# Reordering the HGRN stage of a two-block transformer kernel: gate columns first, query products on VectorE, head pairs staggered, a VectorE matrix-vector product spread through the stage

## The chip, the cores and the metric

The kernel runs on one core of one Trainium2 chip. The metric is device time in microseconds (us) of one execution. TensorE (PE in the rows) does the matrix products, VectorE (DVE), ScalarE (ACT) and GpSimd (POOL) the elementwise work, and SyncE (SP) issues the weight transfers. Each engine runs its own instructions strictly in the order in which they were written.

## What is computed

The reference is two transformer blocks on 256 tokens of width 1024. The change touches only the first mixer of the first block, HGRN2, a gated linear recurrence over 8 heads of 128 key columns:

```python
def hgrn2_mixer(u, w_in, w_out, lb, o_gain):
    q, z_f, v, g = jnp.split(u @ w_in, [...], axis=-1)
    q = jax.nn.silu(q)
    sig = jax.nn.sigmoid(z_f)
    f = lb + (1 - lb) * sig
    log_f = jnp.log(jnp.maximum(f, MIN_FORGET))
    k = (1 - lb) * (1 - sig)
    ...
    attn = jnp.einsum('bthd,btshd,bshd->bhts', qc, decay, kc)
    o = (jnp.einsum('bhts,bshv->bthv', attn, vc)
         + jnp.einsum('bthd,bhdv->bthv', qc * jnp.exp(b), state))
    ...
    o = o * lax.rsqrt(jnp.mean(o * o, axis=-1, keepdims=True) + NORM_EPS) * o_gain
    o = o * jax.nn.silu(g)
    return o @ w_out
```

Beside it the block needs `mod = silu(c) @ mod_w + mod_b`, six matrix-vector products (gemv) of 1024 x 1024 each. The third one (number 2) gates the residual after the mixer, numbers 3 and 4 shift and scale the feed-forward part that follows.

## The kernel before, in words

The core keeps activations transposed (features on partitions, 256 tokens on the free axis) and streams every weight once from memory, in units of 512 KB. A unit is loaded into one of 7 raw buffers by SyncE, then split in two by `emit_conv`: ScalarE casts it to `w_hi` (L193), VectorE subtracts to get `w_lo` (L195), and TensorE multiplies three times for each block, hi·hi, hi·lo and lo·hi (L258 to L260, `mm3`). At most three units are converted ahead of TensorE.

The program is a list of steps, and `run` writes their instructions in the order of the list; before each step `pump` writes the transfers and conversions that have become possible. Nothing is rescheduled afterwards. Inside the HGRN stage the list is the hand-written string `HG_ORDER`. Its names, where the first digit is the pair of heads (0 to 3) and the second a part or level:

- `f20 f21 f30 f31`: gate columns of pairs 2 and 3 on TensorE; `fa fb fc`: their sigmoid in three parts (VectorE, ScalarE, ScalarE `gates_of`). The gates of pairs 0 and 1 come out of the first products (`lin_first`), which stand ahead of `HG_ORDER`, through `ev_f`.
- `d`: `hg_d`, the floor of f at 1e-30 and the product QP = q·f; `t`: `hg_t`, six products of neighbouring f, of neighbouring products and so on, a tree of GpSimd products (L854).
- `s`: `hg_s`, the within-pair products of keys and queries at one of nine levels. Level 8 needs k and q, level 7 needs QP, and the lower levels need keys and queries that `u`, `hg_u`, has scaled with the tree: the key half on GpSimd (L871, L865), the query half on VectorE (L872, L866). So `u06` follows `s07` and precedes `s06`, down to `s00`. `c`: `hg_c`, masked copies of the products of two levels on VectorE.
- `v0` to `v7`: value columns; `w`, `wa wb wc`: output gate; `pv sq st r n m o ol`: products with the values, norm, gate, split in hi and lo; `a0` to `a5`: first part of the output projection.
- `y2x y3x y4x` (x = 0 to 7): the gemv numbers 2, 3 and 4, one 512 KB unit each. 3 and 4 run on TensorE (L523, eight small products). Number 2 runs on VectorE: `gemv_w` multiplies each unit by one column of the condition and adds it to two 128x512 tiles `ga` (L515 for the first unit, L517 for the other seven), and `q2` then sums over partitions on TensorE (L523), `z2` adds the bias.

A `w_lo` conversion that is written behind a waiting instruction on VectorE waits with it, and TensorE then waits for the conversion.

Of the kernel before, what the change touches and what calls it, by code (L numbers as in the profile page):

```python
# [13 lines left out]
AF = mybir.ActivationFunctionType  # L14
OP = mybir.AluOpType
# [31 lines left out]
tr5 o0 y46 y47 pv4 tr6 o1 o2 z3 q4 pv5 pv6 tr7 o3 pv7 z4 o4 o5  # L47
"""
HG_ORDER = """
d0 d1 t0 t1 y30 f20 f21 s08 s18 s07 s17 c00 c10 u06 u16 y31 f30 fa2 s06 s16 u05 u15 y32 fb2 f31 s05 s15 c01 c11  # L50
u04 u14 fc2 y33 v0 fa3 s04 s14 u03 u13 fb3 y34 v1 s03 s13 c02 c12 u02 u12 fc3 d2 y35 v2 s02 s12 u01 u11 d3 t2 t3
y36 v3 s01 s11 u00 u10 s28 s27 s38 s37 y37 v4 s00 s10 u26 u36 c20 c30 z3 v5 s26 s36 u25 u35 pv0 sq0 y40 v6 s25
s35 c21 c31 u24 u34 st0 r0 y41 v7 s24 s34 u23 u33 n0 pv1 sq1 y42 w00 s23 s33 c22 c32 u22 u32 st1 r1 y43 w01 s22
s32 u21 u31 n1 y44 w10 wa0 s21 s31 u20 u30 wb0 y45 w11 wc0 s20 s30 m0 y46 wa1 w20 o0 wb1 ol0 pv2 sq2 wc1 y47 y20
w21 m1 st2 r2 pv3 sq3 z4 y21 w30 o1 ol1 wa2 n2 st3 r3 y22 y23 w31 wb2 wc2 m2 n3 y24 a0 wa3 o2 ol2 wb3 y25 a1 wc3
m3 y26 a2 o3 ol3 y27 a3 q2 a4 z2 a5
"""


# [72 lines left out]
def kernel(ctx: ExitStack, tc: tile.TileContext, x, c, mod_w, mod_b, norm_mix, norm_ffn,  # L132
# [9 lines left out]
    PE, DV, SC, GP, SY = nc.tensor, nc.vector, nc.scalar, nc.gpsimd, nc.sync  # L142
# [24 lines left out]
    def ph(w, name, bufs=2, dt=F32, tag=None):  # L167
        return phase["p"].tile([P, w], dt, name=name, tag=tag or name, bufs=bufs)

    def small(w, name, bufs=2, dt=F32):  # L170
        return wk.tile([P, w], dt, name=name, tag=name, bufs=bufs)
# [464 lines left out]
    st0 = {}  # L636
# [89 lines left out]
    T = {}  # L726
    wa = a_w_in[0]
# [7 lines left out]
        T["v"] = [v[:, 0:D], v[:, D:2 * D]]  # L735

    steps.append(Step(start_hgrn))
    qf, qf_evac, g_steps = [], [], []
    for j in range(4):
        def ev_q(p, j=j):  # L740
            SC.activation(T["q"][:, 2 * j:2 * j + 2].rearrange("p k t -> p (k t)"), p, AF.Silu)
        qf_evac.append(ev_q)
    def gates_of(sg, j):
        for m in range(2):
            h = 2 * j + m
            s_ = sg[:, 256 * m:256 * m + 256]
            if j > 1:
                SC.activation(T["f"][:, h], s_, AF.Identity, bias=lb[:, h:h + 1], scale=one_lb[:, h:h + 1])
                SC.activation(T["k"][:, h], s_, AF.Identity, bias=one_lb[:, h:h + 1], scale=cols[:, 24 + h:25 + h])
                continue  # L750
            DV.tensor_scalar(T["f"][:, h], s_, one_lb[:, h:h + 1], lb[:, h:h + 1], op0=OP.mult, op1=OP.add)
            DV.tensor_scalar(T["k"][:, h], s_, cols[:, 24 + h:25 + h], one_lb[:, h:h + 1], op0=OP.mult, op1=OP.add)

    def pair(n, j):
        return T[n][:, 2 * j:2 * j + 2].rearrange("p k t -> p (k t)")
# [9 lines left out]
    for j in range(2):  # L765
        def ev_f(p, j=j):
            sg = small(512, "sig", 2)
            SC.activation(sg, p, AF.Sigmoid)
            gates_of(sg, j)
        qf_evac.append(ev_f)  # L770
    items = {}
    for j in range(2, 4):
        def ev_f2(p, j=j):
# [19 lines left out]
    def lin_first(h, a, u):  # L793
# [12 lines left out]
        for n in (2 * a, 2 * a + 1):  # L806
# [7 lines left out]
            if h == 3:  # L814
                qf_evac[n](first[n])

    lf = [[Step(lambda u, h=h, a=a: lin_first(h, a, u), [unit_A(wa, 256 * h, (0, 512, 1024)[a], 2, 512)], 2.6)
           for a in range(3)] for h in range(4)]
    for h in range(4):
        steps += [Step(lambda h=h: u0_part(h, LOOK if h == 3 else 1))] + [Step(start_w)] * (h == 3) + lf[h][:1]  # L820
# [17 lines left out]
    DP, QP, SB = {}, {}, {}  # L838

    def hg_d(p):  # L840

        f = pair("f", p)
        DV.tensor_scalar(f, f, 1e-30, None, op0=OP.max)
        QP[p] = ph(512, "qp", 4)
        GP.tensor_mul(QP[p], pair("q", p), f)
        DP[p] = {1: f}

    def hg_t(p):

        d, o = ph(504, "dp", 4), 0  # L850
        for h in (2, 4, 8, 16, 32, 64):
            two = DP[p][h // 2].rearrange("p (n s) -> p n s", s=2)
            DP[p][h] = d[:, o:o + 512 // h]
            GP.tensor_mul(DP[p][h], two[:, :, 0], two[:, :, 1])  # L854
            o += 512 // h
# [120 lines left out]
    def S_(f, *a, cost=1.0):  # L976
        return Step(lambda: f(*a), [], cost)

    def item(key, f, *a):
        items[key] = [S_(f, *a)]  # L980

    LS = ((8, 7), (6, 5), (4, 3))
    for p in range(4):
        for n, f in (("d", hg_d), ("t", hg_t), ("m", hg_m), ("pv", hg_pv), ("sq", hg_sq), ("st", hg_st), ("r", hg_r), ("n", hg_n), ("o", hg_o),
                     ("ol", hg_ol)):
            item(f"{n}{p}", f, p)
        for l in range(9):
# [273 lines left out]
    items = {}  # L1261
# [570 lines left out]
    items = {"sca": [Step(b2_scale)], "col": [Step(b2_cols)], "cx": [S_(c_x)]}  # L1832
# [4 lines left out]
    for i, it in enumerate(mixers):  # L1837
        kind, p = it
# [49 lines left out]
```

## Time and profile before

| what | value |
|---|---|
| time, median of 3 runs (lowest to highest) | 1169.14 us (1168.44 to 1169.78) |
| time of the profiled execution | 1170.95 us |
| span of its trace, first to last instruction | 1169.2 us |
| mean granted TensorE clock | 0.991 of full speed |
| TensorE busy | 1121.8 us (96%) |
| TensorE weight loads | 1037.5 us (89%) |
| VectorE busy | 759.7 us (65%) |
| ScalarE busy | 572.0 us (49%) |
| GpSimd busy | 138.3 us (12%) |
| chain that ended last, share of TensorE | 78% |

The profiled execution lies 1.81 us above the median of the runs. The span is 1.75 us shorter than that execution's own time; what lies outside the trace is not touched by the change. "Busy" of TensorE is modelled, since matmuls overlap; an idle time that the rows give in square brackets is the time from the end of the work before, and behind the arrow stands what ended it. The first products run up to about 68 us of the span, the HGRN stage up to about 211 us. A granted clock of 1.00 is 2.4 GHz, the other level is 1.2 GHz; a stretch that shows 0.61 had some of both.

### The profile page before, as it was taken

To read this page: it belongs to the slowest core of one execution; us is meant where nothing else is said; L and a number is where in the kernel's file an instruction comes from. 1 tells how busy PE (TensorE), PEld (TensorE's weight loads), DVE (VectorE), ACT (ScalarE), POOL (GpSimd) and SP (SyncE) were. 2 spreads that over 40 slices of the span, in tenths; PEclk is the share of its full clock that TensorE was granted. 3 is DMA by queue.
4 is the path that set the end of the run, shared out by engine and by line. 5 is a ranking of instruction groups with operands and counts; after the bars stand their busy time and mean duration, and the time that the engine had idled before them with its cause. 6 is when DMAs were issued, how large, how long until landed. Compare 5 with 4: busy or idle time off the path is not lost.

```text
span 1169.2 us, 23616 instructions
## 1 busy us (share of the span) xinstructions
PE 1121.8 (96%) x9689; PEld 1037.5 (89%) x9689; DVE 759.7 (65%) x1233; ACT 572.0 (49%) x913; POOL 138.3 (12%) x205
## 2 busy tenths in 40 slices
PE   6988998999999999999999999999998999999997
PEld 4976786899999978888999999988898999999997
DVE  3557477677867678885645544666856766766766
ACT  3355263544434556563534434645556544544454
POOL 4035310000000000250000000013322100000000
PEclk9999898999999999999999999999999999999999
DMA  9967467798888767874766555694342656556551
GB/s 275 313 231 232 133 225 242 245 306 292 279 288 287 232 210 247 263 261 145 255 205 199 173 188 173 131 239 127 105 136 83 203 183 212 163 182 198 179 182 54
DMA packets 176124, 241.92 MB, mean 207 GB/s; under 512 B 18712, under 2 KB 142160, under 8 KB 176016
## 3 DMA queue, kind: packets, MB, share of 16 engines
q1 hardware_dynamic: 174928, 239.54, 64.9%
q8 instruction: 76, 1.25, 0.5%
q0 software_dynamic: 912, 0.81, 0.4%
q14 instruction: 32, 0.26, 0.1%
q10 hardware_dynamic: 176, 0.07, 0.0%
HBM read 239.33 MB, written 1.05 MB: 206 GB/s over the span
## 4 chain that ended last, share of the span: by engine, by line
PE 78%; DVE 7%; ACT 5%; DMA 4%; issue 3%; POOL 2%; SPq 0%; DVEq 0%; ACTq 0%; POOLq 0%
PE pb_b L258 14%; PE pb_b L260 14%; PE pb_b L259 14%; PE pb_acc L258 10%; PE pb_acc L260 9%; PE pb_acc L259 9%; DVE w_lo L195 2%; ACT w_hi L193 2%; PE pb_b L462 1%; DMA w_raw<-in_a_w_in_dram 1%; DMA w_raw<-in_kv_w_dram 1%; POOL dp L854 1%; DVE ga L517 1%; PE pb_b L1212 1%; PE pb_gv L523 1%
## 5 line engine op out<-in xcount | busy, mean ns | idle before, releaser
L195 DVE TENSOR_TENSOR w_lo<-w_raw,w_hi 128x1024 fp32r<-128x1024 f32 (+1 forms) x335 | 409.4, 1245 | 180.9 <-ACT w_hi L193 173.4
L258 PE MATMUL pb_b<-s,w_hi 128*128 128x256 f32 x1488 | 424.8, 285 | 5.6 <-ACT s L1746 2.9
L260 PE MATMUL pb_b<-s,w_lo 128*128 128x256 f32 x1488 | 422.1, 284 | 1.5 <-DVE w_lo L195 1.4
L259 PE MATMUL pb_b<-s,w_hi 128*128 128x256 f32 x1488 | 423.0, 284 | 0.4
L193 ACT CAST w_hi<-w_raw 128x1024 fp32r<-128x1024 f32 (+1 forms) x336 | 341.4, 1042 | 82.6 <-DMA w_raw<-in_a_w_in_dram 18.8
L258 PEld LDWEIGHTS pb_b<-s,w_hi 128*128 128x128 f32 x1488 | 285.9, 192 | 13.1 <-issue 4.2
L260 PEld LDWEIGHTS pb_b<-s,w_lo 128*128 128x128 f32 x1488 | 285.9, 192 | 2.6 <-DVE w_lo L195 2.5
L259 PEld LDWEIGHTS pb_b<-s,w_hi 128*128 128x128 f32 x1488 | 285.9, 192 | 2.0 <-DVE s L584 0.7
L258 PE MATMUL pb_acc<-s,w_hi 128*128 128x256 f32 x656 | 190.2, 290 | 0.4 <-ACT w_hi L193 0.4
L260 PE MATMUL pb_acc<-s,w_lo 128*128 128x256 f32 x656 | 186.4, 284 | 1.5 <-DVE w_lo L195 1.5
L259 PE MATMUL pb_acc<-s,w_hi 128*128 128x256 f32 x656 | 186.2, 284 | 0.0
L258 PEld LDWEIGHTS pb_acc<-s,w_hi 128*128 128x128 f32 x656 | 126.2, 192 | 7.0 <-issue 4.6
L260 PEld LDWEIGHTS pb_acc<-s,w_lo 128*128 128x128 f32 x656 | 126.3, 193 | 2.1 <-DVE w_lo L195 2.1
L259 PEld LDWEIGHTS pb_acc<-s,w_hi 128*128 128x128 f32 x656 | 126.3, 193 | 0.4 <-issue 0.2
L1205 POOL TENSOR_SCALAR att<-att,sm 128x128 f32<-128x128 f32 (+1 forms) x72 | 46.5, 662 | 624.4 <-DVE sm L1198 340.7
L1059 ACT CAST s<-sig 128x512 fp32r<-128x512 f32 x38 | 23.6, 620 | 121.2 <-DVE sig L1069 121.2
L258 PE MATMUL pb_acc<-w_hi,s 128*128 128x512 f32 x192 | 77.3, 403 | 2.1 <-ACT s L578 1.0
L259 PE MATMUL pb_acc<-w_lo,s 128*128 128x512 f32 x192 | 75.6, 394 | 0.8 <-DVE w_lo L195 0.8
L260 PE MATMUL pb_acc<-w_hi,s 128*128 128x512 f32 x192 | 75.4, 393 | 0.5 <-issue 0.5
L1772 ACT ACTIVATE sig<-att,vb_t,vc_t 128x256 f32<-128x256 f32 x32 | 17.5, 595 | 77.2 <-DVE att L1767 77.2
L1065 ACT ACTIVATE sig<-pb_b 128x512 f32<-128x512 f32 x22 | 13.1, 597 | 80.6 <-PE pb_b L260 80.6
L1782 POOL TENSOR_TENSOR sig<-sig,rstd 128x512 f32<-128x512 f32 x16 | 22.8, 1427 | 240.2 <-ACT sig L1780 240.2
(372 smaller groups left out, 1258.0 us busy)
## 6 DMA issues: line engine op xcount, KB each, us to landing
w_raw<-in_mod_w_dram SPq DMA_DIRECT2D x96, 512.0 KB, 5.1
w_raw<-in_ffn_w_in_dram SPq DMA_DIRECT2D x88, 512.0 KB, 5.2
w_raw<-in_ffn_w_out_dram SPq DMA_DIRECT2D x44, 512.0 KB, 4.7
w_raw<-in_a_w_in_dram SPq DMA_DIRECT2D x32, 512.0 KB, 5.0
w_raw<-in_ffn_w_gate_dram SPq DMA_DIRECT2D x32, 512.0 KB, 3.7
w_raw<-in_ffn_w_up_dram SPq DMA_DIRECT2D x32, 512.0 KB, 5.3
w_raw<-in_ffn_w_down_dram SPq DMA_DIRECT2D x32, 512.0 KB, 3.5
w_raw<-in_kv_mod_w_dram SPq DMA_DIRECT2D x16, 512.0 KB, 5.7
```

What stands on the lines that cost most here:

```text
L193: SC.copy(hi, raw)
L195: DV.tensor_sub(lo, raw, hi.bitcast(F32))
L258: PE.matmul(o, lhsT=whi, rhs=xhi, start=start, stop=False, skip_group_check=True)
L259: PE.matmul(o, lhsT=whi, rhs=xlo, start=False, stop=False, skip_group_check=True)
L260: PE.matmul(o, lhsT=wlo, rhs=xhi, start=False, stop=stop, skip_group_check=True)
L462: PE.matmul(st[:, 0:256], lhsT=mean_d, rhs=sq[:, 256 * m:256 * m + 256], start=j == 0 and m == 0, stop=j == n - 1 and m == 1)
L517: DV.scalar_tensor_tensor(a, w_, ca[:, k:k + 1], a, op0=OP.mult, op1=OP.add)
L1059: SC.copy(hi, hid)
L1065: SC.activation(sg, g, AF.Silu)
L1205: GP.tensor_scalar(t[:, i, cs], t[:, i, cs], r[:, 2 * b + i:2 * b + i + 1], 1.0, op0=OP.mult, op1=OP.mult)
L1772: SC.activation(zm, am, AF.Identity, bias=vcol("conv_b")[:, f:f + 1], scale=vc_t[:, 64 + f:65 + f])
L1782: GP.tensor_mul(zp, zp, rs_pair())
```

## The change

Gate columns come first in `lin_first`, query columns second and third. The floor of f moves from `hg_d` into `gates_of`, the trees of pairs 0 and 1 are written straight behind the gates (and leave `HG_ORDER`), and the product QP moves from GpSimd to VectorE. `HG_ORDER` is rewritten: `y2` stands first of the three gemv and is done by the time of `y27`, between `w00` and `w01`, `y4` stands last; pair 2 begins its levels while pairs 0 and 1 are at level 2, and pair 3 follows two to three levels behind pair 2, where before 2 and 3 ran level by level together.

```diff
 HG_ORDER = """
-d0 d1 t0 t1 y30 f20 f21 s08 s18 s07 s17 c00 c10 u06 u16 y31 f30 fa2 s06 s16 u05 u15 y32 fb2 f31 s05 s15 c01 c11
...
+d0 d1 y20 f20 f21 s08 s18 s07 s17 u06 u16 y21 f30 fa2 c00 c10 s06 s16 u05 u15 fb2 y22 f31 s05 s15 c01 c11 u04
...
-    qf, qf_evac, g_steps = [], [], []
-    for j in range(4):
-        def ev_q(p, j=j):
-            SC.activation(T["q"][:, 2 * j:2 * j + 2].rearrange("p k t -> p (k t)"), p, AF.Silu)
-        qf_evac.append(ev_q)
+    qf_evac = []
     def gates_of(sg, j):
...
             DV.tensor_scalar(T["k"][:, h], s_, cols[:, 24 + h:25 + h], one_lb[:, h:h + 1], op0=OP.mult, op1=OP.add)
+        DV.tensor_scalar(pair("f", j), pair("f", j), 1e-30, None, op0=OP.max)
...
             gates_of(sg, j)
+            hg_t(j)
         qf_evac.append(ev_f)
+    for j in range(4):
+        def ev_q(p, j=j):
+            SC.activation(T["q"][:, 2 * j:2 * j + 2].rearrange("p k t -> p (k t)"), p, AF.Silu)
+        qf_evac.append(ev_q)
...
-    lf = [[Step(lambda u, h=h, a=a: lin_first(h, a, u), [unit_A(wa, 256 * h, (0, 512, 1024)[a], 2, 512)], 2.6)
+    lf = [[Step(lambda u, h=h, a=a: lin_first(h, a, u), [unit_A(wa, 256 * h, (1024, 0, 512)[a], 2, 512)], 2.6)
...
     def hg_d(p):
 
-        f = pair("f", p)
-        DV.tensor_scalar(f, f, 1e-30, None, op0=OP.max)
+        DP.setdefault(p, {})[1] = pair("f", p)
         QP[p] = ph(512, "qp", 4)
-        GP.tensor_mul(QP[p], pair("q", p), f)
-        DP[p] = {1: f}
+        DV.tensor_mul(QP[p], pair("q", p), pair("f", p))
 
     def hg_t(p):
 
+        DP.setdefault(p, {})[1] = pair("f", p)
...
+    for p in range(2):
+        del items[f"t{p}"]
```

What the table moves shows best on VectorE, at three places. In the rows, `s_256` holds f, `s_255` k, `s_253` q, `s_254` the output gate; what an instruction waits for on other engines stands in brackets.

VectorE behind the last first products, before:

```order
L195 TENSOR_TENSOR w_lo<-w_raw,w_hi 128x1024 [waits DMAHW4_49,Activation_49]
L195 TENSOR_TENSOR w_lo<-w_raw,w_hi 128x1024 [waits DMAHW5_49,PE_49,Activation_49]
L751 TENSOR_SCALAR s_256<-sig,cols 128x256 [waits Activation_49]
L752 TENSOR_SCALAR s_255<-sig,cols 128x256 [waits DVE_49]
L195 TENSOR_TENSOR w_lo<-w_raw,w_hi 128x1024 [waits DMAHW7_49,PE_49,Activation_49]
L843 TENSOR_SCALAR s_256<-s_256 128x512 [waits DVE_49] x2
```

and of the change:

```order
L747 TENSOR_SCALAR s_256<-sig,cols 128x256 [waits Activation_49]
L748 TENSOR_SCALAR s_255<-sig,cols 128x256 [waits DVE_49]
L749 TENSOR_SCALAR s_256<-s_256 128x512 [waits DVE_49]
L195 TENSOR_TENSOR w_lo<-w_raw,w_hi 128x1024 [waits DMAHW4_49,Activation_49]
L195 TENSOR_TENSOR w_lo<-w_raw,w_hi 128x1024 [waits DMAHW5_49,PE_49,Activation_49]
L195 TENSOR_TENSOR w_lo<-w_raw,w_hi 128x1024 [waits DMAHW7_49,PE_49,Activation_49]
L846 TENSOR_TENSOR qp<-s_253,s_256 128x512
L515 TENSOR_SCALAR ga<-w_raw,ca 128x512 [waits DMAHW3_49]
```

The gates (eight of L747 and L748, and two floors, L749) stood behind the conversions of `f20` and `f21`; now they stand ahead of them, and the products QP and the first unit of gemv 2 follow.

VectorE at level 2 of pairs 0 and 1 (`u02 u12` up to `u01 u11`), before:

```order
L872 TENSOR_TENSOR qp<-qp,dp 128x16x16 x2
L843 TENSOR_SCALAR s_256<-s_256 128x512
L195 TENSOR_TENSOR w_lo<-w_raw,w_hi 128x1024 [waits DMAHW5_49,Activation_49]
L195 TENSOR_TENSOR w_lo<-w_raw,w_hi 128x1024 [waits DMAHW6_49,Activation_49]
L872 TENSOR_TENSOR qp<-qp,dp 128x8x32 [waits DVE_49,PE_49] x2
```

and of the change:

```order
L873 TENSOR_TENSOR qp<-qp,dp 128x16x16 x2
L749 TENSOR_SCALAR s_256<-s_256 128x512 [waits Activation_49]
L846 TENSOR_TENSOR qp<-s_253,s_256 128x512
L517 SCALAR_TENSOR_TENSOR ga<-w_raw,ca,ga 128x512 [waits DMAHW2_49]
L195 TENSOR_TENSOR w_lo<-w_raw,w_hi 128x1024 [waits DMAHW7_49,Activation_49]
L873 TENSOR_TENSOR qp<-qp,dp 128x8x32 [waits DVE_49,PE_49] x2
```

The floor here was that of pair 2, whose f was long there; it is now that of pair 3, which waits for ScalarE's `fc3`, and the product QP of pair 2, which `s27` needs, stands behind it. On TensorE `s28 s27` now stand between `v2` and `s02 s12`.

VectorE during the output projection, before:

```order
L959 TENSOR_TENSOR s_256<-s_256,s_254 128x512 [waits DVE_49]
L517 SCALAR_TENSOR_TENSOR ga<-w_raw,ca,ga 128x512 [waits DMAHW1_49]
L195 TENSOR_TENSOR w_lo<-w_raw,w_hi 128x1024 [waits DMAHW6_49,PE_49,Activation_49]
L969 TENSOR_TENSOR olo<-s_256,ohi 128x512 [waits Activation_49]
L517 SCALAR_TENSOR_TENSOR ga<-w_raw,ca,ga 128x512 [waits DMAHW3_49,DVE_49]
L195 TENSOR_TENSOR w_lo<-w_raw,w_hi 128x1024 [waits DMAHW2_49,PE_49,Activation_49]
```

and of the change:

```order
L791 TENSOR_TENSOR s_254<-s_254,sq 128x512
L960 TENSOR_TENSOR s_256<-s_256,s_254 128x512 [waits DVE_49]
L499 TENSOR_TENSOR mod_80<-pb_b,va_t 128x8 [waits PE_49]
L195 TENSOR_TENSOR w_lo<-w_raw,w_hi 128x1024 [waits DMAHW6_49,Activation_49]
L970 TENSOR_TENSOR olo<-s_256,ohi 128x512 [waits Activation_49]
L195 TENSOR_TENSOR w_lo<-w_raw,w_hi 128x1024 [waits DMAHW2_49,PE_49,Activation_49]
```

All 16 instructions of gemv 2 have left this part; the conversions are what is left between the last head pair's gate and its split.

## Rows read from the trace of the kernel before

**Rows 1.** Waits of TensorE, 59 to 217 us: total us, times, longest us.
```profile
PE pb_b L523 <- DVE ga L517: 3.4, 1, 3.4
PE pb_b L894 <- POOL qp L845: 2.6, 2, 1.8
PE pb_b L900 <- POOL s L865: 2.5, 1, 2.5
PE pb_b L894 <- DVE qp L872: 2.1, 2, 1.6
PE pb_b L907 <- DVE qp L872: 1.7, 1, 1.7
PE pb_acc L260 <- DVE w_lo L195: 1.2, 2, 0.8
PE pb_acc L258 <- DVE s L784: 0.9, 1, 0.9
```

**Rows 2.** Stretches: length, busy us and count by engine, clock, DMA share, GB/s.
```profile
72.00:128.00 56.00, 45.84 (x854) 36.33 (x856) 31.96 (x61) 23.54 (x41) 31.49 (x52) 0.91 0.54 178
168.00:200.00 32.00, 26.34 (x188) 23.57 (x187) 26.65 (x36) 15.83 (x22) 0.94 (x1) 0.89 0.76 251
80.00:84.00 4.00, 4.00 (x22) 4.00 (x23) 0.00 (x0) 0.00 (x0) 3.31 (x12) 0.61 0.50 151
120.00:124.00 4.00, 3.75 (x12) 3.30 (x13) 0.35 (x2) 0.52 (x2) 0.71 (x1) 0.50 0.02 4
192.00:200.00 8.00, 6.63 (x35) 5.35 (x35) 3.20 (x5) 2.26 (x3) 0.00 (x0) 0.57 0.76 257
```

**Rows 3.** Timeline behind the first products: start us, length us, instruction.
```profile
65.09 1.08 ACT L741 ACTIVATE s<-pb_acc 128x512 f32<-128x512 f32 x2
67.14 1.22 DVE L195 TENSOR_TENSOR w_lo<-w_raw,w_hi 128x1024 fp32r<-128x1024 f32 x1 [2.31 <-ACT w_hi L193]
68.45 0.28 PE L260 MATMUL pb_b<-s,w_lo 128*128 128x256 f32 x1
70.97 0.42 DVE L751 TENSOR_SCALAR s<-sig,cols 128x256 f32<-128x256 f32 x1 [0.69 <-ACT sig L768]
73.25 0.40 DVE L752 TENSOR_SCALAR s<-sig,cols 128x256 f32<-128x256 f32 x1
74.70 0.75 DVE L843 TENSOR_SCALAR s<-s 128x512 f32<-128x512 f32 x2
```

**Rows 4.** Timeline of levels 8 to 3 of pairs 0 and 1.
```profile
75.28 3.66 POOL L845 TENSOR_TENSOR qp<-s,s 128x512 f32<-128x512 f32 x2 [57.03 <-DVE s L843]
79.59 1.66 POOL L854 TENSOR_TENSOR dp<-dp 128x128 f32<-128x128 f32 x5
...
88.46 0.97 DVE L758 TENSOR_SCALAR s<-s 128x512 f32<-128x512 f32 x1
...
96.78 1.20 DVE L872 TENSOR_TENSOR qp<-qp,dp 128x256 f32<-128x256 f32 x2
...
99.17 0.75 PE L894 MATMUL pb_b<-qp,s 128*32 128x32 f32 x63
```

**Rows 5.** Timeline of level 2 of pairs 0 and 1.
```profile
102.95 0.39 PE L260 MATMUL pb_acc<-w_hi,s 128*128 128x512 f32 x1
103.60 0.72 PE L913 MATMUL pb_b<-qp,s 128*32 128x32 f32 x29 [0.26 <-DVE qp L872]
103.71 0.42 DVE L843 TENSOR_SCALAR s<-s 128x512 f32<-128x512 f32 x1
105.01 0.60 ACT L749 ACTIVATE s<-s,cols 128x256 f32<-128x256 f32 x1
```

**Rows 6.** Timeline of GpSimd, the tree of pair 2.
```profile
113.01 2.78 POOL L854 TENSOR_TENSOR dp<-dp 128x128 f32<-128x128 f32 x5
```

**Rows 7.** Timeline of VectorE in the output projection.
```profile
188.89 0.69 DVE L959 TENSOR_TENSOR s<-s,s 128x512 f32<-128x512 f32 x1
189.50 1.41 DVE L517 SCALAR_TENSOR_TENSOR ga<-w_raw,ca,ga 128x512 f32<-128x512 f32 x2
```

More of the change, by code (lines that the diff above doesn't have):

```diff
@@ L49 @@
 HG_ORDER = """
-d0 d1 t0 t1 y30 f20 f21 s08 s18 s07 s17 c00 c10 u06 u16 y31 f30 fa2 s06 s16 u05 u15 y32 fb2 f31 s05 s15 c01 c11
[L51 to L56, printed above, removed]
+d0 d1 y20 f20 f21 s08 s18 s07 s17 u06 u16 y21 f30 fa2 c00 c10 s06 s16 u05 u15 fb2 y22 f31 s05 s15 c01 c11 u04
+u14 fc2 y23 y30 v0 fa3 s04 s14 u03 u13 fb3 y31 v1 s03 s13 c02 c12 u02 u12 fc3 d2 y32 y24 v2 s28 s27 s02 s12 u01
+u11 u26 t2 y33 v3 s01 s11 u00 u10 c20 s26 u25 d3 y34 v4 s00 s10 s38 s37 u36 s25 u24 t3 y35 y25 v5 pv0 sq0 c21
+s24 u23 c30 s36 u35 y36 v6 st0 r0 s23 u22 s35 u34 y37 y26 v7 n0 pv1 sq1 c22 s22 u21 c31 s34 u33 z3 w00 st1 r1
+s21 u20 s33 u32 y27 y40 w01 n1 s20 c32 s32 u31 y41 w10 wa0 s31 u30 pv2 sq2 wb0 y42 q2 w11 wc0 s30 st2 r2 m0 wa1
+y43 w20 o0 wb1 ol0 pv3 sq3 n2 wc1 y44 z2 w21 m1 st3 r3 y45 w30 o1 ol1 wa2 n3 y46 w31 wb2 wc2 m2 y47 a0 wa3 o2
+ol2 wb3 a1 wc3 m3 z4 a2 o3 ol3 a3 a4 a5
 """
```

## The prediction

> **What bounds the kernel now.** I began with the page: TensorE is busy for 96% of the span, so the change can win only what TensorE loses inside the HGRN stage. The second view was TensorE's waits in that stage [rows 1]. They have three owners: the query side of the pair products, made by GpSimd (2.6 us) or VectorE (2.1 and 1.7 us); the GpSimd update behind two trees (2.5 us); and, at the end, the last sum of gemv 2 on VectorE (3.4 us) with smaller waits for conversions and a gate copy beside it (1.2 and 0.9 us). The third view was the table of stretches [rows 2]. It shows a second price: behind three of these waits the granted clock is 0.61, 0.50 and 0.57 of full speed, that is, TensorE fell for a while to its lower level of 1.2 GHz after it had stood still. What that costs I take as busy time times the missing share of the clock. The same table shows VectorE at 31.96 of 56 us in the first part of the stage and at 26.65 of 32 us in the last. The change moves VectorE work from the full part to the part that is half empty. The timelines [rows 3 to 7] give the single durations.
>
> **The sum, part by part.** Negative is a gain; each TensorE wait is on the path, since the stage has no slack for it.
>
> 1. *Query products and early gates.* The products QP of pairs 0 and 1 hold GpSimd for 3.66 us [rows 4], and TensorE waits 2.6 us for them [rows 1]. On VectorE such a product is a 128x512 product of two tiles, 0.69 us [rows 7]; the two stand ahead of `s07` while TensorE has `f20` and `f21` to do. The wait goes, and with it the slow stretch from 80 to 84 us, 4.00 x 0.39 = 1.6 us [rows 2]. Together -4.2.
> 2. *Trees.* They now run during the gates instead of behind QP, so the first updates are no longer late: -2.1 (the pair products that wait for VectorE's first updates, which started late because GpSimd's clearing of their masks stood behind the trees) [rows 1].
> 3. *A new wait at `f20`.* The sigmoids take the place on ScalarE of the first query activations, so the first is done at about 65.6 us (65.09 plus half of 1.08) [rows 3]. Then eight gates, which took 2.68 us (70.97 to 73.65), two floors, 0.75 us, and only then the conversion of `f20`, 1.22 us [rows 3]: it is ready at 65.6 + 2.68 + 0.75 + 1.22 = 70.3 us. TensorE gets there at about 68.7 us (its last first product starts at 68.45, and two products of `f20` need only `w_hi`), and waits 1.6 us. That is the lower end. Beside GpSimd a 128x512 instruction on one tile took 0.97 us [rows 4] where it took 0.42 us alone [rows 5]; if all five gate and floor instructions of pair 1 meet the tree of pair 0 that is 5 x 0.55 = 2.75 us more, 4.3 us. I take +2.2, near the lower end, because the tree has only some 2.3 us in which to be in the way.
> 4. *Gemv 2 in the first rounds.* A unit costs VectorE 1.41 us [rows 7] ahead of a query update that TensorE waits for. At level 3 the update ended at 97.98 us (96.78 + 1.20) and the products began at 99.17 us [rows 4]: 1.2 us are to spare, so 0.2 us shows. In rounds where gemv 3 has left TensorE the spare time is smaller too. For three such rounds the bounds are 0 and 3 x 1.41 = 4.2 us; I take +1.5, nearer the row.
> 5. *`s27` behind `fc3`.* This is the place at which the new order costs most. The floor of pair 3 waits for ScalarE's last gate, which ended at 105.6 us (105.01 + 0.60) [rows 5], and QP of pair 2 stands behind it on VectorE: ready at 105.6 + 0.42 + 0.69 = 106.7 us. TensorE has finished `v2` by about 103.3 us (102.95 + 0.39) [rows 5] and `s28` by some 103.6 us. It waits 3.1 us where now it waits 0.3 us: +2.8. Behind it are queued `s02 s12`, the next value unit and, on VectorE, gemv 2, a conversion and the updates of level 1. The bounds are 0 (if pair 2's product comes in time after all) and 3.1 plus a slow stretch like that at 120 us, 1.9, so 5.0 us.
> 6. *Levels 1 and 0.* `s01` waited 1.7 us because two conversions stood ahead of its update; now one does. `s00` waited 2.5 us because GpSimd had two trees ahead of its update; now it has one and TensorE has more to do meanwhile. Behind it the slow stretch from 120 to 124 us cost 3.75 x 0.50 = 1.9 us [rows 1, 2]. Together -6.1. What is left of the tree in the way: it may take 2.78 us [rows 6] instead of 1.66 us [rows 4], so 0 to 1.1; I take +0.5.
> 7. *The tail.* All of gemv 2 is gone from the output projection, and its last sum is long done. The waits of 3.4, 1.2 and 0.9 us go [rows 1], and the slow stretch from 192 to 200 us, 6.63 x 0.43 = 2.9 us [rows 2]. Together -8.4. Next in line there is the chain of the last pair's gate and split on VectorE, with six units of projection to cover it.
> 8. *Second half.* The last two units of gemv 2 (2.8 us on VectorE) and the staggered pairs fall where TensorE had no wait at all; cover is VectorE's idle time. The bounds are 0 and 2.8; I take +1.0.
>
> TensorE's own work is the same in both versions, so is the number of transfers. SyncE's queue brings gemv 2 earlier and gemv 4 later; in the first part of the stage only 178 GB/s flow, against 251 and 257 GB/s later [rows 2], so I cost this at nothing there.
>
> Sum: -4.2 - 2.1 + 2.2 + 1.5 + 2.8 - 6.1 + 0.5 - 8.4 + 1.0 = **-12.8 us**. Against the profiled execution's own 1170.95 us that is 1158.2 us; against the median of the runs, 1.81 us lower, **1156.3 us**.
>
> A check from VectorE's side, since it is the engine that is loaded. In the stretch from 72 to 128 us it had 31.96 us [rows 2]. Six units of gemv 2 add about 7.9 us (two multiplications of 0.42, five pairs of 1.41), four QP add 2.8 us, and the gates, which move ahead of 72 us, take 3.4 us away: 39.2 us. My sum makes the stretch 56 - 12.7 + 5.1 = 48.4 us long, so VectorE has to be busy for 81% of it. It was at 83% from 168 to 200 us [rows 2], so it can, but there its instructions waited less for other engines.
>
> The rows of point 3 show that VectorE and GpSimd slow each other: 0.97 against 0.42 us, and the tree's 2.78 against 1.66 us. The Trainium skill, SBUF — State Buffer, "Who interferes with whom", says that the two share one pair of ports, held for a whole instruction, and that the loser is fully blocked rather than slowed. By that rule the gates of pair 1 would stand behind the whole tree of pair 0, so point 3 would be 3.9 and the sum -11.1. The durations that I measured agree in kind.
>
> **Rivals.**
>
> - *The trees and the gates block each other in full.* For: the doubled durations above [rows 4, 6]. Against: QP leaves GpSimd altogether. Each tree is about 2.3 us (five steps are 1.66 [rows 4], the first some 0.6); with both in the way of gates and of the first conversion, point 3 becomes 1.6 + 2.3 + 2.3 = 6.2 us, and TensorE comes out of it at its lower clock, 1.6 us more as from 80 to 84 us [rows 2]. That is 5.6 us worse than the forecast: 1161.9 us.
> - *The new waits are covered.* If `fc3` comes in time and the first rounds hide gemv 2, points 4, 5 and 6 lose their costs and point 5 gains the 0.3: -12.8 - 1.5 - 3.1 - 0.5 = -17.9, or 1151.2 us. Against: the order on VectorE.
> - *Transfers take over the tail.* Gemv 4's units now alternate with the output gate's close to the end. If 251 GB/s is what the transfers can do there, point 7 is given back as a wait for weights: 1156.3 + 8.4 = 1164.7 us. Against: none of the waits of rows 1 is for a transfer.
> - *VectorE becomes the bound, slower than before.* Every microsecond added to VectorE falls on TensorE: gemv 2 and QP, 7.9 + 2.8 + 2.8 = 13.5 us, with 4.3 of point 3, 3.1 of point 5 and two more slow stretches of about 1.8: 24.5 us against gains of 21.1 us (0.3 for the present wait at level 2 included). That is +3.4, or 1172.5 us. It decides from the point where VectorE is filled to less than about 64% in the first part: the stretch may grow by 8.4 - 1.0 - 2.2 = 5.2 us before the kernel is slower, and 39.2 / 61.2 is 64%. Before, it was 57%, with less to do; that is why this case is not small enough to drop.
> - *Nothing moves*: the losses at points 3 to 5 and 8 eat all gains, within 0.2%.
>
> **How the numbers follow.** Forecast 0.50, blocked trees 0.22, covered waits 0.11, transfers 0.06, no change 0.04, slower 0.07. The predicted time is the forecast's. With all costs at their lower ends (1.6, 0, 0, 0, 0) the sum is -19.5 us, 1149.6 us; with all at the upper ends (4.3, 4.2, 5.0, 1.1, 2.8, less 21.1) it is -3.7 us, 1165.4 us. The range 1149 to 1165.5 us takes in these and the first three rivals; it leaves out the last two. 0.2% is about what a measurement of this kernel can tell from no change. Faster by more: 0.50 + 0.22 + 0.11 + 0.06 = 0.89; same 0.04; slower 0.07.
>
> **What would show it.** Right: no TensorE wait for GpSimd's QP and none for the sum of gemv 2, full clock where now 0.61 and 0.57 stand, a tail in which VectorE is well under 83%, a wait at `f20` for its `w_lo` and one of about 3 us at `s27`. Wrong: waits of query products for VectorE in every round of the first part, a slow clock behind the wait at `f20` or `s27`, or a tail in which ScalarE's casts wait for transfers.

## The result, and the profile after

The changed kernel took **1161.49 us** (median of 9 executions, 1158.99 to 1165.31), the kernel before on the same chip 1171.08 us (1168.44 to 1173.95). The ratio is 0.9927, with a 95% interval from 0.9908 to 0.9945: faster by 0.55 to 0.92%, some 6.4 to 10.8 us. The forecast was 1156.3 us, a gain of 12.8. The direction was right and the time lies in the range; the gain is two thirds (8.5 us, by the ratio) to three quarters (9.6 us, by the medians) of the forecast.

The profiled execution took 1159.98 us, its span is 1158.2 us and the mean granted clock 0.995. TensorE's waits in the HGRN stage, 62 to 205 us (total us, times, longest us):

```profile
PE pb_b L895 <- DVE qp L846: 3.1, 1, 3.1
PE pb_b L895 <- DVE cb L925: 2.4, 1, 2.4
PE pb_acc L260 <- DVE w_lo L195: 1.8, 1, 1.8
PE pb_b L497 <- ACT ab L917: 0.9, 1, 0.9
PE pb_b L895 <- ACT ab L910: 0.9, 1, 0.9
PE pb_b L895 <- DVE qp L873: 0.7, 2, 0.4
```

Of the waits of [rows 1] only those for query updates still show, with 0.7 us where they had 3.8 (2.1 and 1.7). The first row is the new wait for QP of pair 2 at `s27`, the third the one at `f20`; both were in the forecast. The second, 2.4 us, was not. The stretches, in the columns of [rows 2]:

```profile
72.00:128.00 56.00, 47.13 (x940) 37.94 (x941) 47.75 (x76) 27.85 (x45) 32.36 (x47) 1.00 0.72 227
128.00:168.00 40.00, 39.00 (x459) 31.35 (x458) 26.43 (x44) 23.29 (x42) 7.11 (x9) 1.00 0.71 222
168.00:200.00 32.00, 32.00 (x284) 29.92 (x284) 18.76 (x27) 15.16 (x21) 0.00 (x0) 1.00 0.75 235
```

The tail is full: TensorE 32.00 of 32 us at full clock, where it was 26.34 at 0.89. VectorE rose from 31.96 to 47.75 us in the first part and fell from 26.65 to 18.76 us in the last. (The windows are fixed in time, and the changed kernel gets through more work in each, so a part of such a difference is work that has moved up.) Where the waits of the first part come from stands in the timeline (start us, length us, instruction; in brackets the idle time before it and what ended it):

```profile
71.05 3.65 POOL L855 TENSOR_TENSOR dp<-dp 128x128 f32<-128x128 f32 x5
...
72.23 2.41 DVE L195 TENSOR_TENSOR w_lo<-w_raw,w_hi 128x1024 fp32r<-128x1024 f32 x2
...
73.54 0.39 PE L260 MATMUL pb_acc<-s,w_lo 128*128 128x256 f32 x1 [1.84 <-DVE w_lo L195]
...
81.66 2.00 DVE L517 SCALAR_TENSOR_TENSOR ga<-w_raw,ca,ga 128x512 f32<-128x512 f32 x2
...
85.59 1.16 DVE L925 COPY_PREDICATED cb<-pairm,pb_b 128x128 f32<-128x128 int32 x4
...
86.36 0.46 PE L895 MATMUL pb_b<-qp,s 128*32 128x32 f32 x32 [2.38 <-DVE cb L925]
...
106.35 0.43 DVE L749 TENSOR_SCALAR s<-s 128x512 f32<-128x512 f32 x1 [1.20 <-ACT s L744]
106.69 0.69 DVE L846 TENSOR_TENSOR qp<-s,s 128x512 f32<-128x512 f32 x1
...
107.43 0.46 PE L895 MATMUL pb_b<-qp,s 128*32 128x32 f32 x32 [3.09 <-DVE qp L846]
```

The products at 86.36 us (`s16`) write a PSUM bank (`pb_b`). A PSUM bank is the piece of memory that the products of this kernel are written to; this one comes free when VectorE has made the masked copies of the first pair squares (`c00 c10`, L925). The new order puts these behind `u06 u16`, a unit of gemv 2, a conversion and a sigmoid part, so they end 2.4 us too late. At 106.35 us the floor of pair 3 waits for ScalarE's gate, QP stands behind it, and TensorE waits 3.09 us, as forecast.

### The profile page after: what moved, and what is told of

Read it like the earlier page. It is cut to its first block, busy times and chain, and to the rows that moved or that the text cites. A ratio compares the mean times of both kernels' runs of the same rounds, so it can differ in the third digit from the quotient of the medians.

```text
span 1158.2 us, 23598 instructions
## 1 busy us (share of the span) xinstructions
PE 1113.7 (96%) x9689; PEld 1032.4 (89%) x9689; DVE 766.3 (66%) x1237; ACT 573.2 (49%) x913; POOL 139.6 (12%) x201
## 4 chain that ended last, share of the span: by engine, by line
PE 82%; DVE 6%; DMA 4%; ACT 4%; issue 2%; POOL 0%; SPq 0%; DVEq 0%; ACTq 0%; POOLq 0%
PE pb_b L258 14%; PE pb_b L260 14%; PE pb_b L259 14%; PE pb_acc L258 11%; PE pb_acc L260 10%; PE pb_acc L259 10%; DVE w_lo L195 2%; ACT w_hi L193 2%; DMA w_raw<-in_a_w_in_dram 1%; PE pb_b L462 1%; DMA w_raw<-in_mod_w_dram 1%; DMA w_raw<-in_kv_w_dram 1%; PE pb_b L1215 1%; PE pb_gv L523 1%; DVE nt L572 1%
## 5 line engine op out<-in xcount | busy, mean ns | idle before, releaser
L259 PEld LDWEIGHTS pb_acc<-s,w_hi 128*128 128x128 f32 x656 | 126.4, 193 | 0.2
```

The lines of the kernel that those rows point to most:

```text
L259: PE.matmul(o, lhsT=whi, rhs=xlo, start=False, stop=False, skip_group_check=True)
```

## The experiments

Each was timed against the kernel before on the same chip, whose median was 1169.95, 1170.95 and 1171.71 us in the three comparisons. "The change" is the changed kernel: 1161.49 us in the result, 1162.75 and 1161.88 us in the two repeats below.

**e0_change_again: the changed kernel, unaltered.**

> The changed kernel once more, beside the kernel before on the same chip, as the base for the runs sent with it. Both theories: 0.991 to 0.994 of the time before. The question is the lead-in: in its profile the first products ended 2.7 us later than before, though nothing ahead of them was reordered. If that belongs to the change (gate columns are fetched in another order), the same delay is seen again; if it is the pace of the first transfers in one execution, the delay is another.

1162.75 us (1159.02 to 1165.09), ratio 0.9931 [0.9912, 0.9951]: the result again. Its profile has the waits of the first one, but 3.8 us and not 3.1 at `s27`, and a slow clock behind that wait (stretches):

```profile
104.00:116.00 12.00, 9.28 (x143) 6.68 (x144) 6.26 (x10) 6.90 (x14) 7.54 (x12) 0.72 0.42 140
```

**e1_gemv_early_alone: the order before, only the gemv units renamed.** Gemv 2 takes the first places of the three, as in the change; the closing steps `q2 z2 z3 z4` move with their units.

```diff
-d0 d1 t0 t1 y30 f20 f21 s08 s18 s07 s17 c00 c10 u06 u16 y31 f30 ...
+d0 d1 t0 t1 y20 f20 f21 s08 s18 s07 s17 c00 c10 u06 u16 y21 f30 ...
...
-m3 y26 a2 o3 ol3 y27 a3 q2 a4 z2 a5
+m3 y46 a2 o3 ol3 y47 a3 a4 z4 a5
```

> Only the order of the three matrix-vector products is changed, all else as before: each place in the order at which one of their units stood keeps a unit, but number 2 (VectorE) takes the early places that the change gives it and number 4 the last ones. Theory of separate parts: the tail's waits and its slow clock go (8.4 us), gemv 2 costs 1.5 to 2.5 us among the first rounds: 6 us faster than before, 1165. Rival, VectorE is already the bound of the first part: the 1.41 us units ahead of the query updates cost about what they cost in the tail, 0 to 2 us faster.

1171.03 us, ratio 0.9999 [0.9983, 1.0014]: nothing, as the rival had it. The waits and the stretches show why:

```profile
PE pb_b L894 <- DVE qp L872: 5.0, 2, 4.6
PE pb_b L900 <- POOL s L865: 4.5, 1, 4.5
PE pb_b L894 <- POOL qp L845: 2.4, 2, 1.5
PE pb_b L497 <- ACT gsb L526: 1.8, 1, 1.8
```

```profile
72.00:128.00 56.00, 40.52 (x739) 33.18 (x738) 39.30 (x70) 24.06 (x41) 31.01 (x50) 0.91 0.58 182
168.00:200.00 32.00, 32.00 (x283) 26.77 (x283) 22.70 (x31) 19.57 (x29) 0.95 (x1) 1.00 0.86 300
```

The tail is as good as that of the change. In the first part TensorE lost 5.3 us of busy time (40.52 against 45.84): the wait for query updates grew from 2.1 to 5.0 us and that for GpSimd's update from 2.5 to 4.5 us. Gemv 2 early moves the loss and doesn't remove it.

**e2_gemv_late: the change, with gemv 2 last again.** Only the units' names differ; their places are those of the change.

```diff
-d0 d1 y20 f20 f21 ...
+d0 d1 y30 f20 f21 ...
...
-... fc3 d2 y32 y24 v2 ...
+... fc3 d2 y36 y37 z3 v2 ...
...
-... u32 y27 y40 w01 ...
+... u32 y47 z4 y20 w01 ...
...
-... wc2 m2 y47 a0 ...
+... wc2 m2 y27 a0 ...
```

> The change with the matrix-vector products in their old order: number 2 stands last again, all else as changed. Theory of separate parts: the changed kernel's time plus 6 us, because the tail has its waits again, less 2 us because the first rounds have VectorE free. Rival (VectorE bounds the first part): the first part gains more than the tail loses, as fast as the changed kernel or faster.

1156.84 us (1155.7 to 1158.25), ratio 0.9876 [0.9856, 0.9895]: 5.9 us better than the change in the same comparison, where the theory of separate parts had it 4 us worse. The wait for the PSUM bank is gone. Even the tail hardly loses (TensorE is busy 30.46 of its 32 us); the last unit of gemv 2 now stands ahead of `a0` and not, as before, between `a2` and `a3`, which is the likely reason. One bad place is left, at `z3` (timeline):

```profile
104.21 0.35 ACT L526 COPY gsb<-pb_gv 128x256 f32<-128x256 f32 x1
...
104.62 0.69 PE L497 MATMUL pb_b<-early,gsb 128*128 128x128 f32 x2 [4.26 <-ACT gsb L526]
...
105.96 0.63 PE L260 MATMUL pb_acc<-w_hi,s 128*128 128x512 f32 x1
106.38 0.63 PE L258 MATMUL pb_acc<-w_hi,s 128*128 128x512 f32 x1
```

The copy of the gemv's sums stands behind four gate parts on ScalarE, TensorE waits 4.26 us for it, and the products behind start 0.42 us apart where 0.23 us is usual.

**e3_code_without_order: the code edits of the change with the order before** (less `t0 t1`).

```diff
-d0 d1 t0 t1 y30 f20 f21 ...
+d0 d1 y30 f20 f21 ...
```

> Gates first, trees at once and QP on VectorE, but with the order of before (gemv 2 last, pairs 2 and 3 level by level together). Theory of separate parts: the waits for QP and the slow clock behind them go (4.2 us), the late updates too (2.1 us), and the wait for the conversion behind the gates comes (1.8 us): 4 to 5 us faster than before. Against the run with gemv 2 late it tells what the staggering is worth: by the sum about 3 us for the staggering; if the wait of 3.1 us behind the last gates eats it, nothing.

1161.01 us (1157.99 to 1164.16), ratio 0.9912 [0.9889, 0.9934]. Gates first, trees at once and QP on VectorE alone are worth as much as the whole change, and twice the 4 to 5 us that were expected. Its largest waits:

```profile
PE pb_b L523 <- DVE ga L517: 3.4, 1, 3.4
PE pb_acc L260 <- DVE w_lo L195: 2.3, 3, 1.1
PE pb_b L908 <- POOL dp L855: 2.0, 1, 2.0
```

The 3.4 us for gemv 2 in the tail are still there. The waits of [rows 1] for query products and for GpSimd's update at `s00` (2.6 and 2.5 us) are gone, the second although both trees still stand ahead of that update: with QP off GpSimd and the floors in the gates it begins at 111.68 us, where before it began at 118.06 us. The 2.0 us stand at `s01`, as the 1.7 us did before. The profile puts them down to a tree step of pair 2, but by the code `s01` does not read that tree; VectorE's update of its queries (L873, from 107.10 us) came just before the products started at 107.70 us. Between e3 and e2 lies the staggered order, 4.2 us (about 3 were expected).

**x1_pair2_before_fc3: `d2` ahead of `fc3`.**

```diff
-... u02 u12 fc3 d2 y32 y24 v2 ...
+... u02 u12 d2 fc3 y32 y24 v2 ...
```

> The change with one token moved: the query product of pair 2 is issued ahead of the last forget-gate step instead of behind it, so it no longer stands behind that pair's floor on VectorE. In the changed kernel TensorE waits 3.1 us for this product. Theory A (a wait in the new order is worth its own length): 2 to 3.1 us less than the change, about 1159.5 us, and the 3.1 us are gone from the waits. Theory B (VectorE is the bound of the first part, so a wait that is removed comes back at its next one): 0 to 1 us less, and the waits for VectorE behind the place grow by about what was removed.

1159.23 us (1158.68 to 1160.83), ratio 0.9902 [0.9887, 0.9917]: 2.3 to 3.5 us less than the change, the time of theory A; the intervals of the two ratios overlap, but all five executions lie below the change's median. The sign of theory A did not come: in the profile the wait fell only from 3.1 to 2.1 us, because QP now stands behind the masked copies of `c02 c12`, and a wait of 1.4 us for a query update came behind it.

**x2_square_copies_early: `c00 c10` ahead of `u06`.**

```diff
-... s07 s17 u06 u16 y21 f30 fa2 c00 c10 s06 ...
+... s07 s17 c00 c10 u06 u16 y21 f30 fa2 s06 ...
```

> The change with the two first copies of the pair squares (c00, c10) back ahead of the query updates of level 6, where they stood before. In the changed kernel the products of level 6 of the second pair wait 2.4 us for a PSUM bank that these copies free. Theory A (the wait belongs to the order of the two): the 2.4 us go and the time falls by 1.5 to 2.4 us against the change. Theory B (VectorE is filled there, so the updates come later by what the copies take): the wait for the bank turns into one for the updates of 1 to 2 us, and the time stays within 0.7 us.

1157.75 us (1157.51 to 1159.54), ratio 0.9891 [0.9876, 0.9906]: 3.7 to 5.0 us less, more than the 2.4 us of the wait. The granted clock of its five executions averages 0.995, that of the change's 0.992. The wait for the bank is gone and nothing took its place (the third row lies behind the stage, and the change has it too):

```profile
PE pb_b L895 <- DVE qp L846: 3.1, 1, 3.1
PE pb_acc L260 <- DVE w_lo L195: 1.8, 1, 1.8
PE pb_b L258 <- ACT s L578: 1.2, 1, 1.2
```

**x6_gemv2_middle_left_out: VectorE skips units 1 to 5 of gemv 2.**

```diff
+            if k in skip:
+                return
...
+        return gemv(*a, 0, skip=(1, 2, 3, 4, 5))
...
-        g = gemv_mod(0, i, gemv_w if i == 2 else gemv)
+        g = gemv_mod(0, i, gemv_s if i == 2 else gemv)
```

> The change with the multiply-and-add pairs of units 1 to 5 of gemv 2 left out on VectorE (their weights are still brought in, TensorE's work is unchanged, so the sum of gemv 2 lacks five of eight units). About 5 x 1.4 to 2.2 = 7 to 11 us of VectorE's work leave the first part of the stage. Theory A (gemv 2 ahead of the updates is what the early spread costs, by VectorE's time): 4 to 6 us less than the change, 1156 to 1158 us, as in the version with gemv 2 late, and the waits for copies and query products shrink. Theory B (the cost is on TensorE: gemv 3 left the first part and with it TensorE's filling, VectorE's load does not matter): the time stays within 1.5 us of the change and the waits stay.

1155.32 us (1153.4 to 1162.59), ratio 0.9878 [0.9854, 0.9902]: 6.2 to 7.4 us less, a little over what theory A gave. TensorE's work is the same, so what gemv 2 costs in the first part is VectorE's time. The wait for the bank shrank to 0.6 us (`PE pb_b L900 <- DVE cb L930`); that at `s27` stayed, at 2.9 us.

**e5_change_third_profile: the changed kernel, a third profile.**

> The changed kernel a third time, to see what differs between its executions, which spread over 6 us. In its first profile TensorE's granted clock was full through the whole stage, in the second it was 0.56 and 0.59 from 104 to 112 us, behind the wait of 3.8 us for the query product of pair 2. Theory A (a wait may or may not be followed by a slow stretch of about 2 us, and that makes the spread): the same waits of 3.1 to 3.8, 2.4 and 1.8 us, slow stretches behind none, one or more of them, and a time that goes up by about 2 us for each. Theory B (the slow stretch follows the wait always, the first profile lost it otherwise): a slow stretch from 104 to 112 us again and nowhere else. Median 1161 to 1163 us by both.

1161.88 us (1160.15 to 1165.29), ratio 0.9921 [0.9898, 0.9944]; the profiled execution took 1164.35 us. The three large waits are as long as in e0 (3.8, 2.4 and 1.8 us). One slow stretch now stands behind the wait for the bank, which in the first two profiles had none; another stands behind the wait at `s27`, as in e0. So theory B, which allowed only the second, falls; in favour of it, two of the three waits at `s27` have such a stretch (stretches, then timeline):

```profile
84.00:96.00 12.00, 9.62 (x172) 8.49 (x171) 7.20 (x12) 3.84 (x6) 3.43 (x4) 0.72 0.50 162
104.00:116.00 12.00, 8.21 (x126) 6.10 (x127) 8.46 (x19) 6.58 (x15) 4.46 (x5) 0.86 0.60 189
```

```profile
87.37 0.66 PE L895 MATMUL pb_b<-qp,s 128*32 128x32 f32 x32 [2.38 <-DVE cb L925]
...
88.76 0.41 PE L258 MATMUL pb_acc<-s,w_hi 128*128 128x256 f32 x1
88.98 0.41 PE L259 MATMUL pb_acc<-s,w_hi 128*128 128x256 f32 x1
...
111.07 0.65 PE L895 MATMUL pb_b<-qp,s 128*32 128x32 f32 x32 [3.79 <-DVE qp L846]
```

The wait for the bank is 2.38 us as in the first profile. There the products behind it lasted 0.28 us and started as little as 0.12 us apart, here 0.41 and 0.21 us.

**x4_three_waits_mended: the three waits taken out by order alone.** `c00 c10` as in x2, `d2` ahead of `c02 c12`, and the gates and tree of pair 1 one step later, so that the conversion of `f20` comes ahead of them.

```diff
-            gates_of(sg, j)
-            hg_t(j)
+            def gates():
+                gates_of(sg, j)
+                hg_t(j)
+            if j == 0:
+                gates()
+            else:
+                late_gates.append(gates)
...
+        if h == 3 and a == 1:
+            late_gates.pop()()
```

> The change with three of its waits taken out by order alone: the square copies c00 and c10 ahead of the updates of level 6 (wait of 2.4 us), the query product of pair 2 ahead of the copies c02 and c12 (wait of 3.1 us), and the gates and the tree of pair 1 behind the conversion for f20 (wait of 1.8 us). Nothing of VectorE's work is removed; gemv 2 stays early. Theory A (waits of order, each worth its length and, where one follows, its slow stretch): 6 to 9 us less than the change, 1153 to 1156 us, a little under 1157.8 us of the version with only the copies moved. Theory B (VectorE is the bound of the first part with gemv 2 in it): no better than 1157 us, other waits for VectorE of 2 us or more in place of those removed.

1155.41 us (1153.55 to 1158.89), ratio 0.9868 [0.9844, 0.9892]: 6.5 us less than the change, within theory A. But something of theory B shows: what is left are waits for query updates in round after round, behind the units of gemv 2, 2.5 us in sum where the change had 0.7, and later ones of 2.1 and 1.3 us (timeline):

```profile
87.51 0.77 PE L902 MATMUL pb_b<-qp,s 128*32 128x32 f32 x61 [0.66 <-DVE qp L880]
...
92.69 0.77 PE L902 MATMUL pb_b<-qp,s 128*32 128x32 f32 x61 [0.95 <-DVE qp L880]
...
97.70 0.76 PE L902 MATMUL pb_b<-qp,s 128*32 128x32 f32 x61 [0.76 <-DVE qp L880]
```

**e4_query_product_on_gpsimd: QP on GpSimd again.**

```diff
-        DV.tensor_mul(QP[p], pair("q", p), pair("f", p))
+        GP.tensor_mul(QP[p], pair("q", p), pair("f", p))
```

> The change with one part undone: the query products are made by GpSimd again, behind the two trees. By the forecast's first point the products on VectorE are worth 4.2 us: 2.6 us of a wait for GpSimd and 1.6 us of slow clock. Theory A (this point holds): 2.5 to 6 us more than the change, 1164 to 1168 us, with a wait of 2.5 us or more for the query product of GpSimd at s08 or s18. Theory B (VectorE is the bound, so that 2.8 us taken from it give back what the wait costs): within 1.5 us of the change.

1161.89 us (1159.07 to 1165.15), ratio 0.9922 [0.99, 0.9945], the same as the change, the time of theory B. The trees now start at 69.9 us, so GpSimd has both products by 81.2 us, and TensorE doesn't wait for them in this profile (timeline):

```profile
78.69 2.54 POOL L846 TENSOR_TENSOR qp<-s,s 128x512 f32<-128x512 f32 x2
```

```profile
80.99 0.75 PE L895 MATMUL pb_b<-qp,s 128*32 128x32 f32 x62
```

But TensorE came late there, through a slow stretch (first row below). From the end of its wait at `f20` (73.20 us) to `s08` (80.41 us) it took 7.2 us, in the three profiles of the change 5.7. Without that 1.5 us it would have waited for GpSimd's second product by some 1.4 us, an estimate from these rows. At `s27`, on the other hand, the wait of 3.1 to 3.8 us is gone: on GpSimd QP of pair 2 (103.57 to 104.86 us) doesn't stand behind the floor of pair 3. A wait of 2.0 us came instead a little later (second row below). So the equal times don't show that the engine of QP makes no difference; they show gains and losses that cancel.

```profile
72.00:80.00 8.00, 6.80 (x44) 6.80 (x45) 5.72 (x6) 5.09 (x6) 7.45 (x11) 0.79 0.70 216
...
PE pb_b L914 <- DVE qp L873: 2.0, 1, 2.0
```

**x5_late_order_mended: e2 with `d2` ahead of `fc3` and `z3` four units later.**

```diff
-... u02 u12 fc3 d2 y36 y37 z3 v2 s28 s27 s02 s12 u01 u11 u26 t2 ...
+... u02 u12 d2 fc3 y36 y37 v2 s28 s27 s02 s12 u01 u11 u26 z3 t2 ...
```

> The version with gemv 2 late, with two tokens moved: the last step of gemv 3 (z3) four units later, and the query product of pair 2 ahead of the last forget-gate step. In the version with gemv 2 late TensorE waits 4.3 us at z3 for ScalarE's copy of the gemv's sums, and the twelve products behind it run at 0.43 instead of 0.23 us each (2.4 us). Theory A (the wait is one of order only): 4 to 7 us less than that version, 1150 to 1153 us. Theory B (ScalarE and VectorE are late there anyway, and TensorE would wait for the last gates or the query product instead): 0 to 2 us less, 1155 to 1157 us, with a wait of 3 to 4 us for the query product in its place.

1153.51 us (1152.0 to 1154.47), ratio 0.9848 [0.9833, 0.9864]: 3.3 us less than e2, between the theories. The 4.3 us are gone, and no wait at `s27` took their place (0.2 us); at its new place `z3` waits 1.9 us for a bank.

**x7_late_order_z3_later: x5 with `z3` behind `v3`.**

```diff
-... u26 z3 t2 y40 v3 s01 ...
+... u26 t2 y40 v3 z3 s01 ...
```

> The mended version with gemv 2 late, with the last step of gemv 3 (z3) moved once more, two units later, behind the fourth value unit. In the mended version it waits 1.9 us for a PSUM bank that ScalarE's copies of pair squares hold. Theory A (order only): the wait goes, 1 to 2 us less, 1151.5 to 1153 us. Theory B (the bank is wanted by whatever comes next): the wait moves to the next product that takes a bank, and the time stays within 0.7 us of 1153.5 us.

1152.81 us (1151.21 to 1154.63), ratio 0.9843 [0.9819, 0.9867]: the fastest median, but x5 can't be told from it by these executions. The 1.9 us are gone from its profile, and the first part shows full clock:

```profile
72.00:128.00 56.00, 52.72 (x1068) 41.48 (x1069) 38.62 (x66) 28.59 (x47) 30.89 (x48) 1.00 0.75 245
```

TensorE is busy 52.72 of 56 us in the first part, 5.6 us more than in the change, with 9 us less of VectorE's work beside it.

**All profiles on one scale.** The stage runs from VectorE's copy L482 (61.88 us before) to its last residual product L622 (211.14 us before), the same two instructions in every kernel. "Waits" is the sum of TensorE's waits in it; "slow clock" is TensorE's busy time times the missing share of the clock, added up over pieces of 4 us; the rest is what remains. All in us:

| kernel | stage | waits | slow clock | rest | median time |
|---|---|---|---|---|---|
| before | 149.3 | 16.0 | 6.7 | 126.5 | 1169.95 to 1171.71 |
| e1, gemv early alone | 148.6 | 17.1 | 5.9 | 125.6 | 1171.03 |
| e3, code alone | 139.3 | 9.8 | 3.1 | 126.4 | 1161.01 |
| the change, first profile | 135.7 | 10.0 | 0.0 | 125.7 | 1161.49 |
| the change, e0 | 138.1 | 10.8 | 2.5 | 124.9 | 1162.75 |
| the change, e5 | 139.6 | 10.7 | 4.0 | 124.9 | 1161.88 |
| e4, QP on GpSimd | 139.1 | 9.6 | 4.7 | 124.9 | 1161.89 |
| x1 | 136.2 | 9.4 | 1.2 | 125.5 | 1159.23 |
| x2 | 135.5 | 8.2 | 1.4 | 125.9 | 1157.75 |
| e2, gemv late | 135.9 | 9.8 | 2.8 | 123.3 | 1156.84 |
| x6, part of gemv 2 left out | 135.1 | 7.5 | 2.8 | 124.8 | 1155.32 |
| x4, three waits mended | 132.9 | 7.2 | 0.0 | 125.7 | 1155.41 |
| x5 | 132.3 | 6.7 | 1.3 | 124.3 | 1153.51 |
| x7 | 130.2 | 5.9 | 0.0 | 124.3 | 1152.81 |

The rest is nearly constant, 123.3 to 126.5 us: to within some 3 us waits and slow clock account for the stage. One profile is one execution, so a row can stand 2 to 3 us off its kernel's median; the three rows of the change show by how much.

## Why the prediction came out as it did

**The waits were counted right in sum.** The forecast has 14.4 us of waits removed and 8.0 us of new ones (2.2 + 1.5 + 2.8 + 0.5 + 1.0), net -6.4. The three profiles show -6.0, -5.2 and -5.3. That the sum agrees is in part luck: the 2.4 us for the bank were not in it, while points 3 and 4 show less wait than was said, and point 8 came by another wait (below).

**The term that was mis-sized is the slow clock.** It stood in points 1, 6 and 7 with 1.6 + 1.9 + 2.9 = 6.4 us, all counted as won, and at nothing behind the new waits: point 5 named "a slow stretch like that at 120 us, 1.9" for the upper bound only. Measured were gains of 6.7, 4.2 and 2.7 us in three executions of one kernel, because a wait of 2.4 or of 3.1 to 3.8 us is followed by a slow stretch in one execution and by none in the next. Of this kind of loss the change won 4.5 us on average of these profiles, not 6.4. A slow clock behind `s27` was one of the prediction's own signs of being wrong, and e0 and e5 have it.

Even 4.5 is on the high side, since the profile of before is a single one and two of the three profiled executions of the change were among its fastest. The granted clock of each execution is on record: it averages 0.9902 in the 38 of the kernel before in the three comparisons and 0.9919 in all 21 of the change. Times the span that is some 11.5 and 9.4 us lost (an estimate; over the whole kernel, and TensorE's idle time included), so about 2 us won. The spread goes with it: in the result the five executions up to 1161.5 us had 0.992 to 0.995, the four from 1163.9 us 0.989 to 0.991. Where in the kernel the clock was low can be seen only in the profiled ones, and not all spread is clock: x4 spreads over 5.3 us at 0.995 to 0.997.

A further part of the shortfall lies outside the sum. The profiled execution of before reached the stage at 61.88 us, the three of the change at 64.61, 63.03 and 65.60 us, all twelve with the new code at 64.1 us on average, e1 with the old code at 63.00 us. The twelve themselves lie between 62.6 and 65.6 us. With two samples of the old code it stays open whether the new order of the first weight units costs 1 to 2 us there or chance does.

Point by point:

1. *Query products and early gates.* The wait of 2.6 us went. Which half of the edit removed it is shown only in part: in e4, with QP on GpSimd, it is nil in the one profile, but by the estimate above some 1.4 us of it would stand there at full clock. So by that estimate the early gates took about half of it and the engine the rest. The move to VectorE also made the wait of point 5, which e4 doesn't have.
2. *Trees.* Right: the wait for the first updates is gone in e3 as in the change, though the five later steps of a tree take 3.65 us (1.66 us in [rows 4]).
3. *`f20`.* 1.8 us, forecast 2.2 within 1.6 to 4.3. The first rival, gates and trees that block each other in full, would have made it 6.2 us. That its time, 1161.9 us, is nearly the measured one is chance.
4. *Gemv 2 in the first rounds.* Mis-sized: +1.5 within 0 to 4.2 was forecast. Leaving it late saves 5.9 us (e2), leaving most of it out 6 to 7 us (x6). The step looked for the cost only where TensorE waits for query updates; those waits are 0.7 us. The rest came through the copies behind it, which hold PSUM banks, 2.4 us and a slow stretch in some executions; x2 takes 3.7 to 5.0 us back by moving them. It takes both, the gemv there and the copies behind it: e2 has the copies in the same place and no such wait. A unit was not 1.41 us there, but 1.8 to 2.2 in four of five.
5. *`s27`.* Forecast 3.1 us, measured 3.1, 3.8 and 3.8. The order made it: x1, with `d2` ahead of `fc3` alone, has 2.1 us, and x4, with `d2` ahead of the copies `c02 c12` too, has none.
6. *Levels 1 and 0.* Right in that the 1.7 and 2.5 us are gone. But the reason given for `s00`, one tree ahead of the update and not two, was not needed: e3 has both and lacks that wait too.
7. *The tail.* Right in size: TensorE 32.00 of 32 us at full clock. But the reason, that all of gemv 2 had to leave, was too strong: in e2 its eight units stand late, from `w01` to just ahead of `a0`, and TensorE is busy 30.46 of 32 us there at full clock.
8. *Second half.* TensorE is busy 39.00 of 40 us where it was 40.00, as forecast +1.0, but that is luck. The wait is not for VectorE's last units of gemv 2; it is that of `z3`, the closing step of gemv 3, for a bank that ScalarE's copies (L917) hold:

```profile
136.90 0.44 PE L497 MATMUL pb_b<-early,gsb 128*128 128x128 f32 x2 [0.92 <-ACT ab L917]
```

The check from VectorE's side forecast 39.2 us of its work in 48.4 us, 81%, which is 45.4 us in 56; it was busy 47.75 us, 85%, with longer single durations: the six units of gemv 2 there took 10.2 us, not 7.9, and of the 3.4 us of gates that the check took away, 1.0 lay ahead of 72 us before as well. The rival that makes it the bound was wrong for the whole change and right for its gemv part: e1, that part alone, gives back all of the tail's gain. In x4 the gemv stays early and 6.5 us come back by order, so it is not the amount of VectorE's work alone.

## What to carry to other kernels

Work that an idle-looking engine takes up is paid for at what stands behind it on that engine: list every instruction behind the moved one for which the bound engine waits, and count copies that free its accumulator banks among them. Placed by that list, two steps of the order moved and the gemv left late (x5) gave 17 us where the change gave 9. Charge a slow-clock share behind new waits as you credit it behind old ones, and look at two or three profiles of one kernel before trusting either.

## What was not expected of the hardware

**The slow clock is not a fixed price of a wait.** The wait of 1.8 us at `f20` left the clock at 1.00 from 72 to 80 us in the three profiles of the change and at 0.79 in x6 and e4, with the wait of the same length; that of 2.4 us for the bank left 1.00 in two profiles and 0.72 from 84 to 96 us in the third. The Trainium skill, TensorE: Matmul & The Clock Gate, "What's actually happening", says of the start of a kernel that the number of slow products varies from run to run. These executions show the same in the middle of one.

**VectorE and GpSimd share the loss.** Five steps of the first tree took 3.65 us (71.05 to 74.70), where they took 1.66 us in [rows 4]. Beside them VectorE had the gates of pair 1 and then two conversions. The five gate and floor instructions of pair 1 took 2.22 us (70.09 to 72.31) where those of pair 0 took 1.72 us (68.46 to 70.18); the two conversions took 2.41 us, no more than the 1.22 us each of [rows 3]. By the rule that the prediction cited, the Trainium skill, SBUF — State Buffer, "Who interferes with whom", the loser of the two is fully blocked. The trace agrees at most instruction by instruction: the gates did not stand behind a whole tree, as the prediction's use of the rule had it, and GpSimd paid most.
